# Adaptive-norm chunks moved between TensorE and VectorE, and a wider norm and split before the feed-forward part

## The chip, the cores and the metric

The program runs on one core of a Trainium2 chip. A core has five engines with a queue of instructions each: TensorE (PE; its weight loads are shown apart as PEld), VectorE (DVE), ScalarE (ACT), GpSimd (POOL) and SyncE (SP), which here issues nearly all DMAs. The metric is the device time of one execution in microseconds (us); several executions give a median.

## The reference, cut to what matters

Two layers work on 640 tokens, 512 latents of one request and 128 context tokens of another, with 1024 features each. Layer 0 has two mixers side by side (A, a bidirectional mLSTM, and B, a Hyena long convolution); layer 1 has neighbourhood attention (mixer C). Around each mixer and each feed-forward part stands the same frame:

```
sh1, sc1, gt1, sh2, sc2, gt2 = split(silu(c) @ w_ada[l] + b_ada[l], 6)   # per layer, c or c_ctx
h = rmsnorm(x, g_mix[l]) * (1 + sc1) + sh1
x = x + gt1 * mixer(h)
a, g = split(rmsnorm(x, g_ffn[l]) * (1 + sc2) + sh2) @ w_up[l], 2)
x = x + gt2 * ((gelu(dwconv3(a)) * g) @ w_down[l])
```

The six vectors of a layer are the "chunks" 0 to 5 of this text: shift, scale and gate of the mixer (0, 1, 2), shift, scale and gate of the feed-forward part (3, 4, 5). Each is a product of a 2-row matrix (c and c_ctx) with 1024 x 1024 weights. The feed-forward width is 2816 = 22 tiles of 128. All arithmetic is fp32.

## The kernel before, in words

**Layout.** Features lie on the 128 partitions in 8 tiles, tokens along the free axis, in two halves of 320 (the first is all latents, the second 192 latents and 128 context tokens, so per-request scalars need two instructions there: RANGES[1]). A normed input is held as a high part XH (rounded to fp32r) and a low part XL (the rest); a product is three matmuls, high by high, high by low, low by high.

**The order of the work.** Engines run their queues in order. The order inside a queue is set by a scheduler of the language from the program's order, its own estimates and explicit marks (`tc.issue_after`); it can push an instruction ahead of ones that stand before it in the code. So a part that is added in one place also moves its neighbours.

**Adaptive-norm chunks.** There are two ways to compute one. `ada_pe` (L212) does it on TensorE, in four steps; a step loads two weight tiles `wa` of 512 KB and runs four matmuls, each on 32 columns of the array, into a PSUM tile `ada`; after the fourth step four small matmuls `adaq` turn the result round. `ada_dve` (L242) does it on DVE, in 16 steps; a step loads one tile `adw` of 256 KB and runs two multiply-and-sum instructions, whose unused product is called `adj` and whose sums go to a tile `ada`; the DVE rows called adj are these. Chunks 0 and 1 of layer 0 run at the start on TensorE, chunks 2, 3, 4 in mixers A and B on TensorE, one step after each of twelve projection tiles (`filler()` at L791, which `linear` calls). Chunk 5 of layer 0 (16 DVE steps, list `early`, L1411) runs in the output projection and the norm after it. Chunks 0 and 1 of layer 1 (32 DVE steps, list `steps`) run in the feed-forward part of layer 0, between the tiles of the down projection: the filler in `ffn_s` (L411) issues by turns two steps and one. Chunks 2 to 5 of layer 1 (64 steps, 8 in each of 8 head pairs) run in mixer C with a single `adw` buffer (L1171, L1348).

**The norm before the feed-forward part.** `norm_part` (L312) treats one feature tile of one half. DVE multiplies x by the coefficient and the broadcast rms factor `rb` into a tile `keep`, ACT adds the shift and rounds to XH, DVE forms XL from keep, shift and XH. In the second half each of these runs twice, on 192 and 128 tokens. Since keep has no shift yet, `shift()` (L463) adds it later on ACT.

**The head of the feed-forward part.** The up projection works by a Strassen-like scheme on sums and differences of the four quarters of the normed input (n11, n21, n12, n22 in keep). `sums()` (L470) forms them between the first three pairs of up tiles (`u_0` to `u_5`, whose low parts are `u_0l` and so on, in PSUM tiles `pu`), and `split_t` (L458) splits four of them, T3, T2, T4 and T1, into a high part by ACT and a low part by a DVE subtraction (128 x 1280 elements each). After the head, `up(f)` (L517) makes seven products per tile f (PSUM tiles A, B, C; their split weights are named `w35wl` for product 3 of tile 5, and so on), a product taking its weights from the loaded tiles `u_5a`, `u_5g`. `down()` (L574) runs four times, the last time at the end; its tiles are `pd`, its residual update writes x. A gate tile `G` and its raw form `gg` lie between up and down.

## Time and profile before

| | us |
|---|---|
| median of 3 runs (range) | 1717.03 (1715.11 to 1718.37) |
| the profiled execution | 1717.35 |
| its span in the trace | 1715.6 |
| busy: PE, DVE, ACT, POOL | 1628.6, 1337.8, 798.5, 147.4 |
| mean granted TensorE clock, share of full | 0.986 |

The stages in the trace: 0 to 75 the start, with filters and first norm; 75 to 217 Hyena and the q/k projection; 217 to 366 the mLSTM; 366 to 412 output projection 0; 412 to 475 the norm and the head of feed-forward 0; 475 to 823 the up and down tiles of feed-forward 0; to 905 its last down, the next norm and the first pair's projection; 905 to 1190 mixer C; 1190 to 1240 output projection 1; 1240 to 1310 norm and head of feed-forward 1; 1310 to 1716 the rest of it. A busy share near 1 for PE in a stage says that work added to TensorE there lengthens the stage; a share well below 1 says that something else ends last there, and the rows of waits say what.

### The profile page before, as it was taken

What the parts mean: (1) busy time and instruction counts of PE and PEld (TensorE: products, weight loads), DVE (VectorE), ACT (ScalarE), POOL (GpSimd) and SP (SyncE); (2) the same over time, 40 slices, a digit from 0 to 9 for tenths busy, and PEclk for the clock granted to TensorE, in tenths of its full rate; (3) what the DMA queues carried; (4) which work ended last, traced back from release to release, by engine and by line L of the source; (5) the groups of instructions that cost most, each with busy time, mean ns of one, the idle gap of its engine ahead of it and who ended that gap; (6) DMA issues with size and microseconds to landing.
All of it is one profiled execution on the core that took longest, in us unless ns stands there. A gap on an engine that the chain in (4) does not pass through costs nothing.

```text
span 1715.6 us, 28580 instructions
## 1 busy us (share of the span) xinstructions
PE 1628.6 (95%) x10978; PEld 1538.9 (90%) x10978; DVE 1337.8 (78%) x2894; ACT 798.5 (47%) x1538; POOL 147.4 (9%) x156
## 2 busy tenths in 40 slices
PE   5999999999799999999997999999988999999997
PEld 2699888999799999999986888888988999999997
DVE  5887556688988989899577777887698597886974
ACT  6323346654542525345355555555274244343542
POOL 3110001101000000000023221220010000000001
PEclk9999999999999999999998999999999999999998
DMA  8335422243214243343323333333311232223231
GB/s 326 111 126 180 148 84 62 61 141 118 69 56 154 82 141 98 92 118 86 97 94 94 102 114 120 101 100 90 117 57 57 67 99 74 87 68 105 75 86 62
DMA packets 69657, 176.71 MB, mean 103 GB/s; under 512 B 9024, under 2 KB 18544, under 8 KB 69264
## 3 DMA queue, kind: packets, MB, share of 16 engines
q1 hardware_dynamic: 69328, 174.71, 32.8%
q8 instruction: 86, 1.41, 0.3%
q14 instruction: 51, 0.42, 0.1%
q0 software_dynamic: 192, 0.17, 0.0%
HBM read 170.65 MB, written 4.20 MB: 102 GB/s over the span
## 4 chain that ended last, share of the span: by engine, by line
PE 78%; DVE 13%; DMA 4%; ACT 3%; issue 2%; POOL 0%; SPq 0%; POOLq 0%; DVEq 0%; ACTq 0%
PE pd L127 14%; PE B L514 11%; PE pqk L127 9%; PE C L514 7%; PE A L514 7%; DMA adw<-in_w_adaT 3%; DVE adj L254 3%; PE pop L127 3%; PE pu L127 2%; PE px L127 2%; PE phyb L127 2%; PE po L127 2%; PE pd L121 1%; PE pS L1317 1%; PE ada L222 1%
## 5 line engine op out<-in xcount | busy, mean ns | idle before, releaser
L349 DVE SCALAR_TENSOR_TENSOR x<-pd,mod,x 128x320 f32<-128x320 f32 (+2 forms) x192 | 73.3, 434 | 107.1 <-PE pd L127 97.3
L254 DVE CUSTOM_DVE_ANT_0 adj<-adw,cbc 128x512 bf16<-128x512 f32 x128 | 96.3, 752 | 38.0 <-DMA adw<-in_w_adaT 36.9
L254 DVE CUSTOM_DVE_ANT_0 adj<-adw,cb 128x512 bf16<-128x512 f32 x96 | 66.1, 689 | 9.4 <-DMA adw<-in_w_adaT 8.0
L564 DVE SCALAR_TENSOR_TENSOR fcb<-fca,cwf,fcb 128x641 f32<-128x641 f32 x76 | 67.1, 884 | 3.0 <-ACT fcb L562 2.6
L1319 ACT COPY pTs<-pS 128x384 f32<-128x384 f32 (+1 forms) x80 | 34.1, 435 | 38.9 <-PE pS L1317 38.4
L1200 ACT ACTIVATE s<-s,nm 128x384 f32<-128x384 f32 x64 | 39.2, 613 | 25.9 <-DVE nm L1305 22.8
L1317 PE MATMUL pS<-ident,s 128*128 128x128 f32 x208 | 36.2, 281 | 13.9 <-DVE s L1202 12.9
L562 ACT ACTIVATE fcb<-fca,cwf 128x641 f32<-128x641 f32 x38 | 31.7, 835 | 34.6 <-DVE fca L519 34.4
L436 ACT ACTIVATE fcb<-fcb 128x641 f32<-128x641 f32 x44 | 32.4, 740 | 30.7 <-DVE fcb L564 30.7
L1382 POOL TENSOR_TENSOR fo<-fo,rs 128x320 f32<-128x320 f32 x8 | 6.9, 896 | 445.0 <-ACT rs L1374 445.0
L288 ACT ACTIVATE sqn<-x 128x320 f32<-128x320 f32 x56 | 25.3, 466 | 40.8 <-DVE x L349 31.9
L1202 DVE TENSOR_SCALAR s<-s,nm 128x384 f32<-128x384 f32 (+1 forms) x80 | 42.9, 543 | 1.2
L1280 POOL TENSOR_TENSOR bm<-amask,wr 128x768 f32<-128x768 f32 x16 | 32.9, 2066 | 118.1 <-issue 91.5
L1317 PEld LDWEIGHTS pS<-ident,s 128*128 128x128 f32 x208 | 23.7, 140 | 20.8 <-DVE s L1202 18.7
L519 DVE TENSOR_TENSOR u<-B,s 128x320 f32<-128x320 f32 x76 | 37.1, 488 | 6.6 <-PE B L514 6.1
L431 ACT CAST G<-gg 128x640 fp32r<-128x640 f32 x44 | 32.0, 728 | 19.9 <-DVE gg L519 17.8
L1305 DVE CUSTOM_DVE_ANT_0 s<-pS,bm 128x384 f32<-128x384 f32 x64 | 34.6, 551 | 8.5 <-PE pS L1304 7.8
L103 POOL TENSOR_TENSOR qk00l<-qk,qk00h 128x1024 fp32r<-128x1024 f32 x1 | 2.8, 2766 | 447.5 <-DVE rn L303 447.5
L1297 PE MATMUL pS<-k,q 128*128 128x256 f32 x128 | 31.0, 329 | 7.6 <-DVE k L1233 7.0
L432 DVE TENSOR_TENSOR G<-gg,G 128x640 fp32r<-128x640 f32 x44 | 36.1, 820 | 1.7 <-ACT G L431 1.6
L519 DVE TENSOR_TENSOR gg<-gg,fcb 128x512 f32<-128x512 f32 x76 | 33.8, 487 | 2.8 <-ACT fcb L436 2.4
L289 DVE TENSOR_TENSOR accn<-accn,sqn 128x320 f32<-128x320 f32 x56 | 30.8, 555 | 6.1 <-ACT sqn L288 5.3
(2003 smaller groups left out, 6136.2 us busy)
## 6 DMA issues: line engine op xcount, KB each, us to landing
adw<-in_w_adaT SPq DMA_DIRECT2D x112, 256.0 KB, 2.9
wa<-in_w_ada SPq DMA_DIRECT2D x40, 512.0 KB, 5.0
d<-in_w_down SPq DMA_DIRECT2D x48, 320.0 KB, 2.8
qk<-in_w_qkv SPq DMA_DIRECT2D x24, 512.0 KB, 3.7
d<-in_w_down SPq DMA_DIRECT2D x16, 448.0 KB, 3.3
u<-in_w_up SPq DMA_DIRECT2D x12, 512.0 KB, 3.7
qk<-in_w_ab SPq DMA_DIRECT2D x8, 512.0 KB, 3.6
op<-in_w_oab SPq DMA_DIRECT2D x6, 512.0 KB, 3.6
```

What stands on the lines that cost most here:

```text
L127: pe.matmul(bank(pt, a)[:, : sp_[a][1] - sp_[a][0]], ww[:, kt], xx[:, slice(*sp_[a])], start=(first and n == 0), stop=(last and n == 2))
L254: dve.tensor_tensor_reduce(out=jk, in0=w, in1=cb[:, s, c], op0=ALU.mult, op1=ALU.add, scale=1.0, scalar=0.0, accum_out=got[0][:, k, h, s : ...
L349: r = dve.scalar_tensor_tensor(out=x[:, k, c0:c1], in0=bank(pt, h)[:, c0 - h * HT : c1 - h * HT], scalar=mod[:, l, ch, k, s : s + 1], in1= ...
L432: here[0] = dve.tensor_tensor(out=g[:, 1], in0=pr, in1=g[:, 0].bitcast(F32), op=ALU.subtract).ins
L514: pe.matmul(o, ww[:, k], xx[:, k], start=(first and k == 0 and n == 0), stop=(last and k == 3 and n == 2), skip_group_check=not first)
L519: tt = lambda o, a, b, op: dve.tensor_tensor(out=o, in0=a, in1=b, op=op)
L564: dve.scalar_tensor_tensor(out=o, in0=av[:, d : d + T + 1], scalar=w[j], in1=o, op0=ALU.mult, op1=ALU.add)
L1200: act.activation(out=s, in_=src, func=AF.Exp, scale=-1.0, bias=nm, accum_out=sm)
L1202: return dve.tensor_scalar(out=s, in0=s, scalar1=sm, scalar2=None, op0=ALU.mult).ins
L1305: dve.tensor_tensor_reduce(out=s, in0=pS[:, 0:384], in1=bm[e][:, (0, 1, 1, 2)[i]], op0=ALU.add, op1=ALU.min, scale=1.0, scalar=3.0e38, acc ...
L1317: pe.transpose(pS[:, j * P : (j + 1) * P], s[:, j * P : (j + 1) * P], ident)
L1319: act.copy(out=t[:, : nk * P], in_=pS[:, : nk * P])
```

## The change

It has five parts. (1) In the second half of the norm before the feed-forward part, DVE multiplies x by rb over all 320 tokens, ACT applies coefficient and shift in place on 192 and 128 tokens, ACT copies the 320 to XH, DVE subtracts over 320. keep of that half then carries its shift, and `shift()` is only for the first half. (2) The low parts of T3, T4 and T1 come from ACT writing minus the high part and an accumulating DMA of 640 KB, issued by POOL, adding the source; T2 stays on DVE. (3) The filler of feed-forward 0 issues two steps on each call. (4) Chunk 5 of layer 0 leaves the DVE list `early` and runs as a fourth `ada_pe` chunk in mixers A and B, with one more `filler()` call after q/k tiles 5, 3, 2 and 6. (5) Feed-forward 0 runs chunks 0, 1 and 2 of layer 1 (48 steps, where it had 32), mixer C chunks 3, 4, 5 (48 steps, where it had 64; 6 in a pair, where it had 8).

```diff
     def norm_part(l, which, nrm, a, rb, ks, keep=None):
         n = 2 * l + which
         for k in ks:
+            if keep and a:
+                t = keep[2 + k // 4][:, k % 4]
+                c = slice(HT, T)
+                dve.tensor_tensor(out=t, in0=x[:, k, c], in1=rb[:, :HT], op=ALU.mult)
+                for c0, c1, s in RANGES[1]:
+                    u = t[:, c0 - HT : c1 - HT]
+                    act.activation(out=u, in_=u, func=AF.Identity, scale=coefA[:, n, k, s : s + 1],
+                                   bias=mod[:, l, 3 * which, k, s : s + 1])
+                act.copy(out=XH[:, k, c], in_=t)
+                last = dve.tensor_tensor(out=XL[:, k, c], in0=t, in1=XH[:, k, c].bitcast(F32), op=ALU.subtract)
+                continue
...
         def filler(st=None):
             every[0] += 1
             st = steps if st is None else st
-            for _ in range(1 + every[0] % 2 if st is steps else 2):
+            for _ in range(2):
...
-        def split_t(dst, src):
+        def split_t(dst, src, by_dma=True):
             act.copy(out=dst[0], in_=src)
-            dve.tensor_tensor(out=dst[1], in0=src, in1=dst[0].bitcast(F32), op=ALU.subtract)
+            if by_dma:
+                act.activation(out=dst[1], in_=dst[0].bitcast(F32), func=AF.Copy, scale=-1.0)
+                pool.dma_start(out=dst[1], in_=src, accum_op=ALU.add)
+            else:
+                dve.tensor_tensor(out=dst[1], in0=src, in1=dst[0].bitcast(F32), op=ALU.subtract)
...
-            shift(2)
-            shift(3)
+            shift(0)
             tt(n22, n22, n12, ALU.subtract)
             split_t(T3, n22)
-            shift(0)
             yield
+            shift(1)
             tt(n12, n12, n11, ALU.subtract)
             tt(n11, n22, n11, ALU.add)
-            split_t(T2, n11)
-            shift(1)
+            split_t(T2, n11, False)
...
-            steps = [ada_pe(0, ((ch, 0), (ch, 1)), hw, "adr", 2, modp, "adasb") for ch in (2, 3, 4)]
+            steps = [ada_pe(0, ((ch, 0), (ch, 1)), hw, "adr", 2, modp, "adasb") for ch in (2, 3, 4, 5)]
...
                 linear(W(13 + j), lambda i, pt, _: done_qk(j, pt), f"qk{j}", head=0, filler=filler)
+                if j in (5, 3, 2, 6):
+                    filler()
...
-            steps = [q for ch in (2, 3, 4, 5) for q in ada_dve(1, ch, at, 1, cb)]
+            steps = [q for ch in (3, 4, 5) for q in ada_dve(1, ch, at, 1, cb)]
...
-                        if 1 <= n <= 8:
+                        if 1 <= n <= 6:
...
-                early = ada_dve(0, 5, pools[1], 2, cb)
-                steps = [q for ch in (0, 1) for q in ada_dve(1, ch, pools[1], 2, cb)]
+                steps = [q for ch in (0, 1, 2) for q in ada_dve(1, ch, pools[1], 2, cb)]
```

On TensorE, in the q/k projection, a step of `ada_pe` stood whole between two tiles before (`pqk` are the tiles' PSUM, `wa` the chunk's weights, XH and XL the input):

```order
L127 MATMUL pqk_1668<-XH,qk50l 128x320 x2
L222 MATMUL ada_1725<-wa_1726,csil 32x512
L222 MATMUL ada_1725<-wa_1727,csil 32x512
L222 MATMUL ada_1725<-wa_1726,csil 32x512
L222 MATMUL ada_1725<-wa_1727,csil 32x512
L127 MATMUL pqk_1740<-XH,qk30h 128x320 x2
```

The next step of the changed kernel, 24 matmuls later in the same tile:

```order
L127 MATMUL pqk_1748<-XH,qk30l 128x320 x2
L222 MATMUL ada_1725<-wa_1734,csil 32x512
L127 MATMUL pqk_1748<-XH,qk30h 128x320 x2
L127 MATMUL pqk_1748<-XL,qk30h 128x320 x2
L127 MATMUL pqk_1748<-XH,qk30l 128x320
L222 MATMUL ada_1725<-wa_1735,csil 32x512
L222 MATMUL ada_1725<-wa_1734,csil 32x512
L222 MATMUL ada_1725<-wa_1735,csil 32x512
```

The step is now two groups, of one and of three matmuls, with five matmuls of the tile between. Of the 16 steps of chunks 2 to 5, nine stay whole and seven are split like this.

On DVE, at the end of the first down projection and the begin of the next up tiles, before (the x rows are the residual of the last down tile, the rows L254 are the chunk's steps, `w35wl` is the low part that product 3 of tile 5 waits for):

```order
L349 SCALAR_TENSOR_TENSOR x<-pd_0_7_1_5342,mod,x 128x128
L254 ISA adj_5378,ada_5028<-adw_5376,cb_3448 128x512
L254 ISA ada_5028 128x1
L519 TENSOR_TENSOR u_6a<-ss_6_5426,u_6a 128x512
L254 ISA adj_5380,ada_5028<-adw_5376,cb_3448 128x512
L254 ISA ada_5028 128x1
L507 TENSOR_TENSOR w35wl<-u_5a,w35wh 128x512
```

And in the changed kernel:

```order
L360 SCALAR_TENSOR_TENSOR x<-pd_0_7_1_5288,mod,x 128x128
L530 TENSOR_TENSOR u_6g<-u_6a,u_6g 128x512
L254 ISA adj_5324,ada_4950<-adw_5322,cb_3490 128x512
L254 ISA ada_4950 128x1
L530 TENSOR_TENSOR gg_5_4907<-B_5_4812,s_5_4791 128x320
L254 ISA adj_5326,ada_4950<-adw_5322,cb_3490 128x512
L254 ISA ada_4950 128x1
L530 TENSOR_TENSOR u_6a<-ss_6_5374,u_6a 128x512
L254 ISA adj_5330,ada_4950<-adw_5328,cb_3490 128x512
L254 ISA ada_4950 128x1
L518 TENSOR_TENSOR w35wl<-u_5a,w35wh 128x512
```

Between the last residual and `w35wl` stand three adj where there were two, and `u_6g` and `gg_5` besides; two more adj stand among the three parts of that residual, which had none. Counted from the first adj of this down projection, 31 adj come ahead of `w35wl`, where 22 did.

On DVE, in the head of feed-forward 0, the low part of the fifth up tile, `u_4l`, stood behind two gate products, two gate subtractions and a token sum:

```order
L455 TENSOR_TENSOR gg_0_4374<-pu_1_4221,fcb_4194 128x2x128
L452 TENSOR_TENSOR gg_1_4466<-pu_3_0_4416,fcb_4195 128x320
L452 TENSOR_TENSOR gg_1_4466<-pu_3_1_4417,fcb_4195 128x192
L452 TENSOR_TENSOR gg_1_4466<-pu_3_1_4417,fcb_4195 128x128
L432 TENSOR_TENSOR G_0_4377<-gg_0_4374,G_0_4377 128x640
L472 TENSOR_TENSOR keep_3444<-keep_3447,keep_3444 128x1280
L432 TENSOR_TENSOR G_1_4470<-gg_1_4466,G_1_4470 128x640
L103 TENSOR_TENSOR u_4l<-u_4_4481,u_4h 128x1024
```

In the changed kernel it stands right behind the first gate product:

```order
L466 TENSOR_TENSOR gg_0_4309<-pu_1_4156,fcb_4129 128x2x192
L466 TENSOR_TENSOR gg_0_4309<-pu_1_4156,fcb_4129 128x2x128
L103 TENSOR_TENSOR u_4l<-u_4_4401,u_4h 128x1024
L443 TENSOR_TENSOR G_0_4312<-gg_0_4309,G_0_4312 128x640
L463 TENSOR_TENSOR gg_1_4386<-pu_3_0_4336,fcb_4130 128x320
```

So `gg_1`, both `G` and one sum of 1280 elements moved behind `u_4l`.

## Rows read from the trace of the kernel before

**Rows 1.** Page, part 4: shares of the chain that ended last.

```profile
PE 78%; DVE 13%; DMA 4%; ACT 3%; issue 2%; POOL 0%; SPq 0%; POOLq 0%; DVEq 0%; ACTq 0%
```

**Rows 2.** Stages: window, length, busy (count) of PE, PEld, DVE, ACT, POOL, clock, DMA, GB/s.

```profile
75.00:217.00 142.00, 141.83 (x990) 126.26 (x989) 106.39 (x192) 42.14 (x77) 9.64 (x4) 1.00 0.44 149
412.00:475.00 63.00, 51.39 (x318) 49.03 (x318) 58.22 (x128) 39.12 (x75) 5.11 (x3) 0.95 0.25 76
475.00:823.00 348.00, 346.65 (x2347) 344.04 (x2346) 314.95 (x644) 149.47 (x251) 0.00 (x0) 1.00 0.35 105
905.00:1190.00 285.00, 262.35 (x1965) 238.49 (x1963) 225.67 (x588) 154.03 (x362) 65.05 (x46) 0.98 0.35 107
1240.00:1310.00 70.00, 60.99 (x391) 58.67 (x390) 63.42 (x128) 43.83 (x86) 8.19 (x15) 0.95 0.17 54
```

**Rows 3.** Timeline of PE: start, duration, line, operation, out<-in; TensorE chunk groups.

```profile
49.73 0.31 PE L121 MATMUL phya<-XH,hya0l 128*128 128x320 f32 x1
49.97 1.06 PE L222 MATMUL ada<-wa,csil 128*32 128x512 f32 x6
50.95 0.41 PE L121 MATMUL phya<-XL,hya0h 128*128 128x320 f32 x1
51.20 0.31 PE L118 MATMUL phya<-XH,hya1h 128*128 128x320 f32 x1
...
52.47 1.04 PE L222 MATMUL ada<-wa,csil 128*32 128x512 f32 x2
...
177.20 0.95 PE L230 MATMUL adaq<-selc,adasb 128*128 128x4 f32 x8
```

**Rows 4.** Loads of the tile wa between 75 and 217 us: landing times.

```profile
DMA to landing us min/median/max: 3.5/4.4/6.3
```

**Rows 5.** Timeline of PE in head 0, rows that had idle before them.

```profile
432.99 0.41 PE L118 MATMUL pu<-XH,u_0h 128*128 128x320 f32 x1 [1.88 <-ACT XH L324]
...
462.41 0.56 PE L127 MATMUL pu<-XH,u_4l 128*128 128x320 f32 x2 [4.46 <-DVE u_4l L103]
```

**Rows 6.** First down projection: stage of all engines, then adj alone on DVE.

```profile
511.00:547.00 36.00, 36.00 (x248) 36.00 (x247) 29.05 (x74) 7.17 (x11) 0.00 (x0) 1.00 0.51 151
...
511.00:547.00 36.00, 13.77 (x20) 1.00 0.51 151
```

**Rows 7.** Timeline of the first down and its end: DVE, then PE.

```profile
531.09 0.69 DVE L254 CUSTOM_DVE_ANT_0 adj<-adw,cb 128x512 bf16<-128x512 f32 x1
...
531.83 0.69 DVE L254 CUSTOM_DVE_ANT_0 adj<-adw,cb 128x512 bf16<-128x512 f32 x1
...
549.94 0.69 DVE L507 TENSOR_TENSOR w35wl<-u_5a,w35wh 128x512 fp32r<-128x512 f32 x1
...
550.69 0.41 PE L514 MATMUL C<-XH,w35wl 128*128 128x320 f32 x1
```

**Rows 8.** Page, part 6: DMA issues, KB each, median us to landing.

```profile
adw<-in_w_adaT SPq DMA_DIRECT2D x112, 256.0 KB, 2.9
...
u<-in_w_up SPq DMA_DIRECT2D x12, 512.0 KB, 3.7
```

**Rows 9.** Waits between 905 and 1190 us.

```profile
DVE adj L254 <- DMA adw<-in_w_adaT: 31.8, 24, 3.1
...
PE pS L1317 <- DVE s L1202: 12.9, 16, 1.3
```

**Rows 10.** Timeline of PE in head 1, and the stage behind its wait.

```profile
1293.94 0.90 PE L127 MATMUL pu<-XH,u_4l 128*128 128x320 f32 x2 [4.31 <-DVE u_4l L103]
...
1292.60:1299.40 6.80, 5.46 (x20) 5.46 (x21) 6.80 (x7) 1.97 (x2) 0.00 (x0) 0.50 0.35 91
```

**Rows 11.** ACT cast of T1, and the first matmul of PE that reads its low part.

```profile
473.63 1.26 ACT L459 CAST XH<-keep 128x1280 fp32r<-128x1280 f32 x1 [0.68 <-PE pu L127]
...
484.77 0.30 PE L514 MATMUL C<-XL,w53wh 128*128 128x320 f32 x1
```

**Rows 12.** All DMA issues: the one of 1024 KB.

```profile
cb<-in_cond_b SPq DMA_DIRECT2D x1, 1024.0 KB, 6.4
```

More of the change, by code (lines that the diff above doesn't have):

```diff
@@ L456, in done_up @@
             gate(f, pr)
-        def split_t(dst, src):
+        def split_t(dst, src, by_dma=True):
             act.copy(out=dst[0], in_=src)
-            dve.tensor_tensor(out=dst[1], in0=src, in1=dst[0].bitcast(F32), op=ALU.subtract)
+            if by_dma:
[3 more added lines that the diff above has]
+                dve.tensor_tensor(out=dst[1], in0=src, in1=dst[0].bitcast(F32), op=ALU.subtract)
         def shift(i):
-            a = i // 2
             for k in range(4):
-                for c0, c1, s in RANGES[a]:
-                    t = keep[i][:, k, c0 - a * HT : c1 - a * HT]
-                    act.activation(out=t, in_=t, func=AF.Identity, bias=mod[:, l, 3, 4 * (i % 2) + k, s : s + 1])
+                t = keep[i][:, k]
+                act.activation(out=t, in_=t, func=AF.Identity, bias=mod[:, l, 3, 4 * i + k, 0:1])
         def sums():
@@ L1527, in pack @@
     wa = i["w_ada"]
-    o["w_ada"] = wa[0].reshape(4, 2, P, 6, 2, 512)[:, :, :, :5].transpose(3, 0, 4, 2, 1, 5).reshape(5, 4, 2, P, 1024)
+    o["w_ada"] = wa[0].reshape(4, 2, P, 6, 2, 512).transpose(3, 0, 4, 2, 1, 5).reshape(6, 4, 2, P, 1024)
     o["w_adaT"] = wa.reshape(2, D, 6, KT, P).transpose(0, 2, 3, 4, 1).reshape(12, KT, P, D)[5:]
```

## The prediction

> **What bounds the kernel now.** I read the chain of waits first, then the stages, then the waits inside the stages that the change touches. The chain lies on TensorE for 78% and on DVE for 13% [rows 1]: work added to TensorE should mostly lengthen the run, and work added to DVE should matter where the stage has no slack. The stages say where that is [rows 2]. From 75 to 217 us TensorE is busy 141.83 of 142 us: nothing can be hidden there. From 475 to 823 it is busy 346.65 of 348, but DVE is busy 314.95 as well, so TensorE bounds the stage with DVE some 10% behind. In the two heads (412 to 475 and 1240 to 1310) TensorE stands idle for 63 - 51.39 = 11.6 us and 70 - 60.99 = 9.0 us, and its mean granted clock there is 0.95, worth about 5% of the stage, 3.2 and 3.5 us. In mixer C it is idle for 285 - 262.35 = 22.6 us. So the change takes work out of stages in which TensorE waits, and puts it into a stage in which TensorE bounds and one in which DVE nearly does. The sum is made against the profiled execution, 1717.35 us; the median is 1717.03, so 0.3 is taken off at the end.
>
> **Mixers A and B: a fourth chunk on TensorE.** The rows show what a group of such matmuls costs between two neighbours [rows 3]. From 49.73 to 51.20 pass 1.47 us, in which TensorE also starts two projection matmuls. The first down projection starts 248 matmuls in 36 us, 0.145 apiece [rows 6]; 1.47 - 0.29 = 1.18 us for the group. That group has three matmuls (six records, 1.06 us); the one at 52.47 has a single matmul (two records) and takes 1.04 us. Its size doesn't matter, only the number of groups does, since the four column groups run side by side. Before, chunks 2 to 4 were 12 whole steps, 12 groups. After, the order shows 9 whole steps and 7 that are split in two: 23 groups. 11 x 1.18 = 13.0 us. One more round of adaq (0.95 us busy, overlapping its neighbours a little) adds 0.9: 13.9 in all. Two `wa` buffers hold one step, so the loads of a step start only after the last matmul of the one before. For most of the split steps 24 matmuls lie between, 24 x 0.145 = 3.5 us, and a load lands after 3.5 at best, 4.4 in the median [rows 4]. The first group needs only the first of the two tiles, so I take 0.3 us for each of seven such steps, 2 us; the bounds are 0 and, with the median landing, 7 x 0.9 = 6.3. Term: +15.9, from +13.9 to +20. Nothing covers it.
>
> **Norm and head of feed-forward 0.** The ceiling is 11.6 + 3.2 = 14.8 us. The DVE steps of chunk 5 leave this stage, and with them the delay in XH and XL for which TensorE waits (1.88 us in one place [rows 5]). The largest wait, 4.46 us for `u_4l` [rows 5], gets shorter as `gg_1`, two G and one sum move behind `u_4l`. It doesn't go: `gg_0`, still ahead of it, needs the gelu on ACT, and ACT has the negation of T3 to do first, 1.26 us if it is as long as the cast of T1 [rows 11]. I leave 1.8 us of it, and 2.9 for idle of other origin (the first wait for the rms factor, a split on POOL). 14.8 - 4.7 = 10.1. Term: -10, from -5 to -13.
>
> **Low parts by accumulating DMA.** No such DMA stands in the trace. For T3 and T4 DVE is relieved. T1 comes last: its cast ran at 473.63 to 474.9 [rows 11], the negation would end at 476.2, and TensorE first reads the low part at 484.77 [rows 11], 8.6 us later. A load of 512 KB lands in 3.7 us [rows 8] and one of 1024 KB in 6.4 [rows 12]; 640 KB lie between, near 4.4, and up to twice that, 8.8, if reading the destination as well costs as much again. If the head gets shorter by 10 us on TensorE, ACT's cast must move with it. Term for both layers: +1, from 0 to +5. The Trainium skill ("DMA: Bandwidth & Descriptors", section "Anatomy of one DMA — SWDGE (gpsimd) path") fits a DMA issued by GpSimd as 2.0 us plus bytes over 436 GB/s, here an estimate of 3.5 us. "Collectives: The Full Stack" of the Trainium skill (section "The bandwidth ceiling: the fold count and why AG ≠ RS ≠ AR") speaks against the change: an adding DMA reads two sources and so pushes twice the read traffic. By the two together T1 would be an estimate of 5 us, still inside the 8.6, and the term would be 0; no row here shows such a DMA.
>
> **The downs of feed-forward 0.** Feed-forward 0 now carries 48 steps, which is 32 adj more. Two adj back to back start 0.74 us apart [rows 7]; 23.7 us of DVE work. DVE has 348 - 315 = 33 us free in the stage as a whole [rows 2], but not where the work comes: in the first down it is busy 29.05 of 36 us, 13.77 of them in 20 adj [rows 6]. The order says when this shows: 31 adj come ahead of `w35wl`, where 22 did, so `w35wl` comes 9 x 0.74 = 6.7 us later, less what of the free 36 - 29.05 = 6.95 us can be used. Before, it ran 549.94 to 550.6 and the matmul that reads it started at 550.69 [rows 7]: just in time, so each us later is a us of TensorE. The bounds are 0 and 6 for a down. That all the free time can be used is not likely: two steps for a tile of 36/8 = 4.5 us need two loads of 2.9 us [rows 8] through two buffers, and a buffer is taken for 2.9 + 2 x 0.74 = 4.4 us and the issue. I take 2.7 for each of three downs (the third gets 16 steps where it had 8). Term: +8, from 0 to +16.
>
> **Mixer C.** A quarter of the steps goes. DVE waited 31.8 us for `adw` there, in 24 waits, and TensorE 12.9 us in 16 for a DVE row `s` that stands behind such waits [rows 9]. A quarter of it would be 3.2 us, all of it 12.9. I take 7, since two units of each pair have no step at all now. Term: -7, from -3 to -13.
>
> **Norm and head of feed-forward 1.** Ceiling 9.0 + 3.5 = 12.5. `u_4l` cost 4.31 us of waiting, and behind it stand 6.8 us at half clock (1.2 GHz), worth 3.4 [rows 10]. With 1.8 left of the wait and the clock kept up, 2.5 + 3.4 = 5.9; the wide norm saves DVE some instructions in front of TensorE: 1 more. Term: -7, from -2 to -10.
>
> **The sum.** 15.9 - 10 + 1 + 8 - 7 - 7 = +0.9; 1717.35 + 0.9 - 0.3 = 1718. Gains and costs, each over 20 us, nearly cancel.
>
> **Rivals.** *The downs hide it.* DVE uses all its free time in the downs (0 in place of +8), the loads of `wa` come in time (+13.9), and the heads and mixer C give -11, -8 and -9: 13.9 - 11 + 0 + 1 - 9 - 8 = -13, 1704. For it speaks the free 33 us of DVE; against it that 0 for a down needs every idle us. *The DVE queue becomes the bound in feed-forward 0* (slower). Place: the three downs and the up tiles behind them. A tile's DVE work is four adj (3.0), a residual and a weight split; if these pass 4.5 us, or a load through two buffers does, each tile lags, and the lag reaches `w35wl` and its like as 5 us each: +15 in place of +8, 1725. It decides from the point at which DVE shows no idle between residuals. For it speaks 13.77 us for 20 adj in 29.05 busy: twelve more leave nothing. *`wa` is late* (slower): the loads of the split steps land after the median 4.4 us or more beside the projection's own loads; +8 to +10 in mixers A and B: 1725 too. *The split groups don't cost*: if a group of one matmul hid beside its neighbours, mixers A and B would cost four groups, one adaq and the waits, 4.7 + 0.9 + 2 = 7.6 in place of 15.9, and the time be 1710; the row at 52.47 speaks against it.
>
> **How the numbers follow.** I give my forecast 0.37, the downs that hide it 0.25, free split groups 0.05, the DVE bound 0.20, late `wa` 0.13. A measurement of this kernel can tell about 0.2%, 3.4 us, from no change. Of the forecast's 0.37 (its own range 1712 to 1724) 0.25 are within that, 0.06 on either side; the first rival and the free groups give 0.28 to faster and 0.02 to same, the two slow ones 0.29 to slower and 0.04 to same. Faster 0.34, same 0.31, slower 0.35. For 8 in 10 the range reaches to the rivals on both sides: 1703 to 1732.
>
> **What would show it.** Between 75 and 225 us the stage should be 14 to 18 us longer, with groups `ada` of x2 and x6 at about 1.05 us each. The head of feed-forward 0 should show `u_4l` waits under 2 us and no clock of 0.5 behind it. After the pd of each down there should be a wait of TensorE for a low part (`w35wl`) of 2 to 4 us; if there is none, the first rival holds; if it is over 4 or DVE is busy over 97% from 475 to 823, the second. In mixer C the wait for `adw` should fall from 31.8 to about 24 us. The prediction fails if the accumulating DMA lands later than 8 us, or if the norm's second half, now with three ACT instructions per tile, makes TensorE wait for ACT where it waited for DVE.

## The result and the profile after

The changed kernel takes 1731.79 us, median of 4 runs (1729.16 to 1733.87), beside 1717.7 us (1715.11 to 1719.31) for the kernel before: a ratio of 1.0083, 95% interval 1.0068 to 1.0099. It is slower by 0.8%, some 14 us. The forecast was 1718, no change, with a range of 1703 to 1732: the median lies 0.2 us inside its upper end. The profiled execution takes 1729.16 us with a span of 1727.4, against 1715.6: 11.8 us more.

Where they went can be read from the starts of named matmuls on TensorE, since the same groups run in both kernels. A stage here is the time from the first start of one group to the first start of the next (us; "head" is output projection, norm and up head together, from `pop` to the first product A):

| stage, from - to | before | after | change | forecast |
|---|---|---|---|---|
| start, to `phya` | 49.04 | 45.87 | -3.2 | 0 |
| mixers A and B, `phya` to `px` | 202.18 | 221.24 | +19.1 | +15.9 |
| mLSTM, `px` to `pop` | 120.92 | 120.93 | 0 | 0 |
| head 0, `pop` to A | 105.11 | 92.61 | -12.5 | -10 |
| A to the first down | 33.80 | 33.90 | +0.1 | +1 (T1) |
| the first three downs, `pd` to A, each | 35.20 | 35.20 | 0 | |
| up tiles behind them | 63.62, 62.47, 78.03 | 69.96, 69.34, 86.77 | +21.9 | +8 |
| last down, projection C | 83.96 | 84.12 | +0.2 | 0 |
| mixer C, `pv` to `pop` | 302.43 | 295.18 | -7.3 | -7 |
| head 1, `pop` to A | 102.58 | 95.65 | -6.9 | -7 |
| feed-forward 1 to the end | 405.82 | 406.23 | +0.4 | 0 |

One row is far off: the up tiles of feed-forward 0. The stages of the changed kernel that answer to [rows 2], in the same columns (window, length, busy time and count of PE, PEld, DVE, ACT and POOL, clock, DMA, GB/s):

```profile
72.00:220.50 148.50, 146.10 (x972) 124.47 (x972) 103.43 (x186) 40.61 (x75) 9.65 (x4) 0.99 0.45 150
428.00:480.60 52.60, 48.91 (x330) 47.83 (x331) 45.51 (x84) 41.42 (x72) 7.24 (x5) 1.00 0.33 85
480.60:846.20 365.60, 350.24 (x2318) 346.56 (x2317) 330.54 (x703) 147.00 (x248) 0.89 (x1) 0.97 0.39 112
930.30:1214.00 283.70, 267.05 (x2003) 242.77 (x2003) 219.51 (x573) 158.40 (x374) 62.87 (x46) 0.98 0.34 102
1255.00:1321.00 66.00, 62.24 (x411) 60.67 (x410) 52.61 (x98) 46.86 (x81) 9.51 (x6) 0.97 0.26 69
```

In the third row TensorE is now idle 365.6 - 350.24 = 15.4 us, where it was idle 1.35, and its clock is 0.97 where it was 1.00. DVE is busy 330.54 of 365.6, 90%, the same share as before: it is not full. So something makes both wait. The timeline of TensorE shows where: once behind each of the first three downs (start, duration, instruction, idle before it and its releaser):

```profile
559.26 0.63 PE L525 MATMUL B<-TT,w45wh 128*128 128x320 f32 x1 [5.13 <-ACT w45wh L517]
...
663.73 0.90 PE L525 MATMUL B<-TT,w611wh 128*128 128x320 f32 x2 [3.39 <-ACT w611wh L517]
...
769.03 0.90 PE L525 MATMUL B<-TT,w415wh 128*128 128x320 f32 x2 [5.32 <-ACT w415wh L517]
```

The chain of waits between 545 and 565 us of the changed kernel says what ended the first of them (start, duration, what):

```profile
547.67 3.36 DMA adw<-in_w_adaT
551.16 0.69 DVE adj L254
...
553.10 3.01 DMA adw<-in_w_adaT
556.24 0.69 DVE adj L254
557.34 0.49 DVE adj L254
557.95 0.62 DVE u_6a L530
558.59 0.63 ACT w45wh L517
559.26 0.90 PE B L525 x2
```

Read from below: the product waits for ACT's cast, the cast for DVE's row that makes `u_6a`, and that stands behind adj rows which wait for their loads. DVE's own timeline shows these waits (bracketed, as above):

```profile
541.12 0.69 DVE L254 CUSTOM_DVE_ANT_0 adj<-adw,cb 128x512 bf16<-128x512 f32 x1 [1.40 <-DMA adw<-in_w_adaT]
...
551.16 0.69 DVE L254 CUSTOM_DVE_ANT_0 adj<-adw,cb 128x512 bf16<-128x512 f32 x1 [0.65 <-DMA adw<-in_w_adaT]
...
557.87 0.69 DVE L530 TENSOR_TENSOR u_6a<-ss,u_6a 128x512 f32<-128x512 f32 x1
```

There are five of them in this down and the turn behind it, 0.52 + 0.29 + 1.40 + 0.65 + 0.30 = 3.2 us; the other two downs have 3.1 and 3.4 us. Within each wait of TensorE begins a stretch at half clock, which goes on behind it; the stages of these stretches, columns as in [rows 2]:

```profile
556.50:563.30 6.80, 4.04 (x15) 4.04 (x16) 6.46 (x17) 0.71 (x2) 0.00 (x0) 0.50 0.58 175
662.30:669.10 6.80, 5.36 (x19) 4.95 (x20) 5.94 (x19) 4.15 (x7) 0.00 (x0) 0.50 0.32 105
768.10:774.90 6.80, 5.87 (x22) 5.87 (x23) 4.64 (x12) 0.62 (x1) 0.00 (x0) 0.50 0.26 77
```

TensorE is busy 4.04 + 5.36 + 5.87 = 15.3 us in them at 1.2 GHz in place of 2.4, so half of that, 7.6 us, is lost. The idle time grew by about 14.1 us (15.0 us of waits of 0.3 us or more between 546 and 850, less 0.9 in the same place before). 14.1 + 7.6 = 21.7 of the 21.9 us.

In the mixers the groups on TensorE look as [rows 3] let expect, and one load is late:

```profile
188.92 1.05 PE L222 MATMUL ada<-wa,csil 128*32 128x512 f32 x2
190.83 1.06 PE L222 MATMUL ada<-wa,csil 128*32 128x512 f32 x6
...
197.76 1.62 PE L222 MATMUL ada<-wa,csil 128*32 128x512 f32 x2 [2.17 <-DMA wa<-in_w_ada]
```

A group of one matmul (x2: each has two records) and one of three (x6) take the same time. There are 23 groups, as forecast. The last shown ran at half clock (its stretch is 3.4 us long and doesn't stand in the six runs below with the same code, which take 218.8 to 219.3 us for the stage: +17).

In both heads the wait for `u_4l` that [rows 5] and [rows 10] show is down to 1.10 us. No half clock stands behind it in head 0; in head 1 a stretch of 3.4 us does (the last row, columns as in [rows 2]):

```profile
467.64 0.56 PE L127 MATMUL pu<-XH,u_4l 128*128 128x320 f32 x2 [1.10 <-DVE u_4l L103]
...
1306.62 0.56 PE L127 MATMUL pu<-XH,u_4l 128*128 128x320 f32 x2 [1.10 <-DVE u_4l L103]
...
1307.40:1310.80 3.40, 3.40 (x15) 3.40 (x14) 3.40 (x6) 1.94 (x2) 0.00 (x0) 0.50 0.56 154
```

In mixer C the waits that answer to [rows 9] (us in total, times, longest; between 905 and 1225 us) are shorter:

```profile
DVE adj L254 <- DMA adw<-in_w_adaT: 20.9, 23, 1.9
...
PE pS L1330 <- DVE s L1215: 8.9, 13, 1.3
```

And the accumulating DMAs, which no row of before showed, stand in the list of DMA issues with their landing time:

```profile
TT<-keep POOLq DMA_DIRECT2D x4, 640.0 KB, 5.6
XL<-keep POOLq DMA_DIRECT2D x2, 640.0 KB, 6.0
```

The one for T1 of layer 0 is issued at 480.19 and by the median of 6.0 us lands about 486.2; TensorE reads XL of it from 488.27 and waits for nothing.

The 3.2 us at the start are no effect of the change. Stretches of half clock near 36 us come and go there between kernels whose start is the same (before, and the runs e1, e4, e5, e6 and e12 have 6.8 us of it, e7 and e9 have 3.4, the changed kernel and e2, e3, e8 and e11 none). Without the start the traces differ by 15.0 us, near the 14 of the medians.

### The profile page after: what moved, and what is told of

Its sections match the earlier page's. It is cut to its first block, busy times and chain, and to the rows that moved or that the text cites. A ratio compares the mean times of both kernels' runs of the same rounds, so it can differ in the third digit from the quotient of the medians.

```text
span 1727.4 us, 28568 instructions
## 1 busy us (share of the span) xinstructions
PE 1643.4 (95%) x11018; PEld 1543.5 (89%) x11018; DVE 1304.2 (75%) x2792; ACT 804.1 (47%) x1529; POOL 151.1 (9%) x162
## 4 chain that ended last, share of the span: by engine, by line
PE 51%; DVE 14%; DMA 5%; issue 2%; ACT 2%; POOL 0%; POOLq 0%; ACTq 0%; DVEq 0%
PE B L525 11%; PE pd L127 10%; PE C L525 7%; PE A L525 7%; DMA adw<-in_w_adaT 5%; DVE adj L254 4%; PE pqk L127 2%; PE pu L127 2%; PE pu L121 1%; PE pop L127 1%; PE pd L121 1%; DVE s L1215 1%; PE pS L1330 1%; PE py L1345 1%; PE pS L1310 1%
## 5 line engine op out<-in xcount | busy, mean ns | idle before, releaser
L254 DVE CUSTOM_DVE_ANT_0 adj<-adw,cbc 128x512 bf16<-128x512 f32 x96 | 68.6, 715 | 21.8 <-DMA adw<-in_w_adaT 20.9
L254 DVE CUSTOM_DVE_ANT_0 adj<-adw,cb 128x512 bf16<-128x512 f32 x96 | 65.9, 687 | 10.9 <-DMA adw<-in_w_adaT 9.6
L360 DVE SCALAR_TENSOR_TENSOR x<-pop,mod,x 128x320 f32<-128x320 f32 (+2 forms) x36 | 14.3, 433 | 36.7 <-PE pop L127 26.1
L222 PE MATMUL ada<-wa,csil 128*32 128x512 f32 x192 | 39.6, 662 | 2.2 <-DMA wa<-in_w_ada 2.2
```

The lines of the kernel that those rows point to most:

```text
L222: pe.matmul(pt[32 * j : 32 * j + 32, :], cs_[0][:, 2 * kp + par, :], rr[i][:, par * 512 : (par + 1) * 512], start=(kp == 0), stop=(kp == 3))
L254: dve.tensor_tensor_reduce(out=jk, in0=w, in1=cb[:, s, c], op0=ALU.mult, op1=ALU.add, scale=1.0, scalar=0.0, accum_out=got[0][:, k, h, s : ...
L360: r = dve.scalar_tensor_tensor(out=x[:, k, c0:c1], in0=bank(pt, h)[:, c0 - h * HT : c1 - h * HT], scalar=mod[:, l, ch, k, s : s + 1], in1= ...
```

## The experiments

Each was timed 4 to 10 times beside the kernel before on the same chip; ratios are to that kernel, with the 95% interval. The kernel before took 1714.4 to 1717.7 us on these chips, so runs are best compared by their ratios. Stage lengths are from their traces, by the same starts as in the table. All but e1, e3 and e4 have three adw buffers in feed-forward 0, as e2 does.

**e1: the old pace.**

```diff
-            for _ in range(2):
+            for _ in range(1 + every[0] % 2 if st is steps else 2):
                 if st:
```

> The changed kernel with part 3 undone alone: the filler of feed-forward 0 issues two steps and one by turns, so its 48 steps run 12 in each of four downs, the last one included, where the changed kernel puts 16 in each of the first three. Theory (pace): the adj rows of a down stand in DVE's queue ahead of the row that makes u_6a, whose cast TensorE waits for; with 24 adj as in the kernel before they come in time. Then the waits of 5.1, 3.4 and 5.3 us behind the first three downs fall below 0.6 each, the three stretches of half clock behind them go, the up tiles take 62 to 64, 62 to 63 and 78 to 79 us again (from 70.0, 69.4 and 86.8), and the time is about 20 us shorter, 1711. The last down may give back up to 3 us. Rival (load): it is the number of steps in the stage, with its DMA traffic, not the pace: 48 are still there, and most of the 22 us stays, 1727 to 1732.

Measured: 1711.61 us, ratio 0.9981 (0.9968 to 0.9995). The up tiles take 64.1, 61.7 and 79.4 us; the largest wait behind a down is 0.74 us and no half clock stands there. The projection of mixer C, behind the last down that now has steps, takes 35.2 us in place of 31.8: 3.4 us back. The theory held. All 48 steps are still in the stage, so their number is not the cause. The pace is, but this doesn't yet say whether by DVE's work or by the loads.

**e2: three adw buffers, pace as changed.**

```diff
-                steps = [q for ch in (0, 1, 2) for q in ada_dve(1, ch, pools[1], 2, cb)]
+                steps = [q for ch in (0, 1, 2) for q in ada_dve(1, ch, pools[1], 3, cb)]
```

> The changed kernel with three adw buffers in feed-forward 0, where it has two; the pace of two steps for a tile stays. DVE waited for adw in the first down and the turn behind it 0.5 + 0.3 + 1.4 + 0.65 + 0.3 = 3.2 us. Theory (pace): DVE work ahead of u_6a is too long in any case, the loads are a part of it: the waits behind the downs shrink by up to 3 us each but do not go; the time is 4 to 10 us shorter, 1722 to 1728. Rival (loads): the two buffers are the cause, and with three the waits and the half clock behind them go: about 1711.

Measured: 1710.82 us, ratio 0.998 (0.9967 to 0.9993). The up tiles take 64.3, 63.6 and 80.3 us, 4.1 us more than before the change and 17.8 less than with two buffers. In no wait of 0.3 us or more between 475 and 842 does DVE wait for adw. What is left of TensorE's waits behind the first and the third down:

```profile
554.06 0.56 PE L525 MATMUL B<-TT,w45wh 128*128 128x320 f32 x2 [2.40 <-ACT w45wh L517]
...
752.42 0.56 PE L525 MATMUL B<-TT,w415wh 128*128 128x320 f32 x2 [2.39 <-ACT w415wh L517]
```

My theory expected a gain of 4 to 10 us; the rival held. The rows ahead of `u_6a` in DVE's queue cost 2.4 us of wait, which no half clock follows here. The loads cost the rest: 2.7 us more of wait in the first down, 2.9 in the third, and the half clock. A third buffer also changes the order of DVE's queue a little, but not in a way that could explain the gain: 31 adj of the first down stand ahead of `u_6a` in e2, 30 in the changed kernel, and yet `u_6a` starts 5.3 us behind the first product A in e2 and 8.1 in the changed kernel (2.5 before).

**e3: whole groups on TensorE.** The order of the two matmuls that share a half step is turned round.

```diff
-                for i in range(2):
+                for i in (1, 0):
                     j = 2 * par + i
```

> The changed kernel with the two matmuls of each half step of the chunks on TensorE in the other order, so that the first of a step reads the tile that is loaded second; then no step is split, 16 groups where the changed kernel has 23. Theory (number of groups): seven groups less are 7 x 1.18 = 8.3 us; the projection stage, 19 us longer than before in the changed kernel, is 9 to 11 us longer; time 1722 to 1725. Rival (loads): what costs there is waiting for wa, and as a whole step now waits for its second tile, the waits eat the gain: 1728 to 1733.

Measured: 1726.33 us, ratio 1.0069 (1.0046 to 1.0092). All 16 steps are whole, seven groups less, but mixers A and B take 218.9 us, as with split groups. The number of groups alone doesn't set the stage. The stage from `phya` to `px` in the kernel before, e2 and e3, columns as in [rows 2]:

```profile
49.04:251.22 202.18, 202.01 (x1297) 174.15 (x1293) 149.85 (x286) 72.64 (x131) 16.51 (x13) 1.00 0.41 135
...
45.61:264.76 219.15, 216.55 (x1337) 176.48 (x1333) 151.71 (x289) 72.51 (x130) 16.93 (x14) 1.00 0.41 142
...
46.47:265.37 218.90, 210.51 (x1339) 177.28 (x1336) 151.69 (x290) 72.67 (x130) 16.94 (x14) 0.99 0.41 142
```

TensorE's busy time is 6.0 us less in e3 than in e2, and 8.5 less without the 2.5 us that two stretches at half clock cost in e3, close to the 7 x 1.18 = 8.3 us of the seven groups. But its idle time is 8.4 us where e2 has 2.6. It waits three times for wa (1.79, 0.52, 0.57; e2 once, 1.6), and at the stage's end for the gate columns:

```profile
263.28 0.78 PE L990 MATMUL gT<-ident,R 128*128 128x128 f32 x4 [3.71 <-ACT R L978]
```

The gates' first row on ACT, in this kernel, waits for the last Hyena block (`hy`), which stands behind the adaq of the last step:

```profile
240.29 0.80 ACT L934 ACTIVATE gt<-pgates,bgt 128x640 f32<-128x640 f32 x1 [5.11 <-PE hy L875]
```

In the kernel before the same row ran 16 us earlier, and its chain was over before TensorE wanted it. In the changed kernel and in e2 it runs as late as in e3 (243.05 and 240.69), but there TensorE comes to gT later and waits for nothing. So neither expectation holds: the groups' gain is there, and waits that the split groups had hidden take it back. The row of before:

```profile
224.04 0.79 ACT L921 ACTIVATE gt<-pgates,bgt 128x640 f32<-128x640 f32 x1
```

**e4: low parts of the sums on DVE.**

```diff
-        def split_t(dst, src, by_dma=True):
+        def split_t(dst, src, by_dma=False):
```

> The changed kernel with the low parts of T3, T4 and T1 formed by a DVE subtraction again, no accumulating DMA. Theory (the chunk and the wide norm made the heads shorter, the DMA did little): the stretch from output projection 0 to the first product is 92.6 us in the changed kernel, 105.1 before; it gets 1 to 3 us longer; that of layer 1 too (95.7, 102.6 before); time 1733 to 1737. Rival (the DMA gave most of it): each head goes half the way back or more, 5 us and more in sum: over 1738. Second rival (the accumulating DMA costs): it gets faster, below 1730.

Measured: 1727.38 us, ratio 1.0076 (1.0055 to 1.0096), the same as the changed kernel. Head 0 takes 92.5 us, head 1 94.0; 0.7 us is lost behind each head, where TensorE waits 0.45 us for a weight split on DVE. The heads got neither 1 to 3 us longer nor 5 and more. The time is under the 1730 of the second rival, but the kernel before ran 3.3 us shorter here as well (1714.41), and the intervals of the two ratios overlap: the DMAs neither shorten the heads nor cost anything that these runs can tell.

**e5: narrow norm** (part 1 undone: `norm_part`, `shift` and `sums` as before, with the DMAs).

> The changed kernel with three adw buffers in feed-forward 0 and with part 1 undone: the norm's second half in narrow steps again, with the shift of keep added later. Theory (the steps that left shorten the heads): the stretch from output projection to the first product stays within 2 us of the changed kernel's 92.6 and 95.7, and the time within 3 us of the version with three buffers alone. Rival (the wide norm does it): both stretches go back by 3 us or more each, most of the way to 105.1 and 102.6, and the time is 6 us longer or more.

Measured: 1712.23 us, ratio 0.9969 (0.9956 to 0.9983). Heads 94.4 and 95.9, within 2 us. The first theory held.

**e6: chunk 5 on DVE** (part 4 undone).

```diff
-            steps = [ada_pe(0, ((ch, 0), (ch, 1)), hw, "adr", 2, modp, "adasb") for ch in (2, 3, 4, 5)]
+            steps = [ada_pe(0, ((ch, 0), (ch, 1)), hw, "adr", 2, modp, "adasb") for ch in (2, 3, 4)]
...
-                if j in (5, 3, 2, 6):
-                    filler()
...
+                early = ada_dve(0, 5, pools[1], 3, cb)
```

> The changed kernel with three adw buffers in feed-forward 0 and with part 4 undone: chunk 5 of layer 0 runs on DVE in output projection 0 and its norm again. Theory (chunk 5 costs on TensorE what groups, waits and the end of the chain cost, and gives back the head's gain): mixers A and B take 202 us again, 17 less; the stretch behind them goes back from 92.6 to 101 to 105, 8 to 12 more; the time is 5 to 9 us shorter than with three buffers alone. Rival (the wide norm and the DMA have taken over the head's gain): the stretch stays near 93 and the time is 15 us shorter or more.

Measured: 1695.86 us, ratio 0.987 (0.9849 to 0.989), by its median the fastest of all. That is 15 us below e2, the time of the rival, where the theory had 5 to 9; the profiled executions are 10.5 us apart. Mixers A and B take 202.2 us, 17 less; head 0 takes 98.8, 6.2 more, between the two expectations. `u_4l` keeps its early place, and the waits for XH, 2.6 us in two, come back:

```profile
455.74 0.74 PE L127 MATMUL pu<-XH,u_4l 128*128 128x320 f32 x2 [1.09 <-DVE u_4l L103]
```

**e7: whole groups, and the additional steps early.**

```diff
-                if j in (5, 3, 2, 6):
+                if j in (0, 1, 4, 7):
                     filler()
```

> The changed kernel with three adw buffers in feed-forward 0, the whole groups of the run with that name, and the four additional fillers after q/k tiles 0, 1, 4 and 7 instead of 5, 3, 2 and 6, so that the last step of chunk 5 comes where chunk 4's last step came before. In the run with whole groups alone, TensorE waited 3.7 us for the gate columns (gT): the gates' first row on ACT waits for the last Hyena block, which stands behind the last step's adaq. Theory (the end of the chain): with the last step early, that chain starts 15 us or more earlier and is hidden; mixers A and B take 208 to 213 us (219 to 221 in the changed kernel), the time is 6 to 11 us shorter than with three buffers alone. Rival (the loads of wa): two steps in one tile wait for their loads wherever they stand; 216 to 219, and the time stays.

Measured: 1700.93 us, ratio 0.9903 (0.9886 to 0.9919). Mixers A and B take 209.5 us, 9.6 less than in e2; `gt` starts at 228.66, 12 us earlier than in e2 and e3, and gT waits for nothing. The stage, columns as in [rows 2]:

```profile
46.36:255.87 209.51, 207.07 (x1339) 175.44 (x1335) 151.09 (x289) 74.06 (x132) 16.62 (x14) 1.00 0.44 148
```

The first theory held in the length of the stage; the time is 10 us under e2 by the medians and 13 by the ratios, where 6 to 11 were expected. Against e2 the gain is busy time, 9.5 us, that is the groups, at the same idle time of 2.4 to 2.6 us. Against e3, which has whole groups too, the early place alone gives 9.4 us: it takes away the waits. Split groups in the early place weren't tried. Against the 202.2 of before the chunk costs 7.3 us here: four groups and one adaq, 5.1 us of busy time (5.6 by the prices of the forecast), and waits.

**e8: chunk 2 of layer 1 back in mixer C** (part 5 undone).

```diff
-            steps = [q for ch in (3, 4, 5) for q in ada_dve(1, ch, at, 1, cb)]
+            steps = [q for ch in (2, 3, 4, 5) for q in ada_dve(1, ch, at, 1, cb)]
...
-                        if 1 <= n <= 6:
+                        if 1 <= n <= 8:
...
-                steps = [q for ch in (0, 1, 2) for q in ada_dve(1, ch, pools[1], 3, cb)]
+                steps = [q for ch in (0, 1) for q in ada_dve(1, ch, pools[1], 3, cb)]
```

> The changed kernel with three adw buffers and with part 5 undone: feed-forward 0 has 32 steps, mixer C 64 in 8 for each pair. Theory (a quarter of the steps): mixer C takes 300 to 303 us again (295 to 296 with 48 steps), and as its last steps run into output projection 1 and the norm, that stretch goes back to 101 to 103 from 95.7; feed-forward 0 gets 2 to 5 us shorter, and the time is 5 to 11 us longer than with three buffers alone. Rival (the wide norm shortened head 1): mixer C goes back, but the stretch behind it stays at 94 to 96, and the time is 1 to 5 us longer.

Measured: 1722.13 us, ratio 1.0038 (1.0019 to 1.0056), 0.6% above e2's ratio, some 10 us, as the theory had it. Its ten runs spread over 12 us, and the profiled one is the fastest. Mixer C takes 302.4 us again, to 0.1 us what it took before. Head 1 takes 99.1, between the two expectations: 18 adj run in it, as the steps spill over into output projection 1 (before the change 18 too, none in the changed kernel), and TensorE waits 1.7 us for XL and 0.9 for XH there as it did before, but for `u_4l` only 1.1 us. The wait for adw in mixer C goes back as well:

```profile
DVE adj L254 <- DMA adw<-in_w_adaT: 33.4, 25, 3.0
```

**e9: e6 with three steps on a call in output projection 0.**

```diff
         def filler():
-            for _ in range(2):
+            for _ in range(3):
                 if steps:
```

> The version with three adw buffers and chunk 5 on DVE, with one more edit: the filler of output projection 0 issues three steps on a call instead of two, so that more of chunk 5's 16 steps come before the norm. In that version TensorE still waits 1.8 + 0.4 + 0.8 us for XH and XL in head 0. Theory (adj rows left in the norm make these waits): the stretch from output projection 0 to the first product falls from 98.8 us to 95 to 97, the time by 2 to 4 us. Rival (three steps delay the residuals of the output projection, as two through two buffers did in the downs): the stretch gets longer, 99 to 103, and the time by up to 4 us.

Measured: 1698.43 us, ratio 0.9897 (0.9877 to 0.9917), which overlaps e6's interval. Head 0 takes 97.5, 1.25 less, in part because a new wait comes up, 2.02 us of TensorE for the sum of squares on DVE. That is in neither expected range; inconclusive in time, no gain.

**e11: parts 1 and 2 both undone** (e5 with `by_dma=False`).

> The changed kernel with three adw buffers in feed-forward 0, and parts 1 and 2 both undone: narrow norm, all low parts of the sums on DVE. In the runs with one of them undone TensorE waited 1.0 us for u_4l (4.5 and 4.3 before the change, 1.1 with it). In the order of this kernel u_4l still stands right behind the first gate product. Theory (u_4l's place in DVE's queue sets its wait, and parts 1 and 2 matter little for it): it waits 1 to 2 us in both layers, the two stretches up to the first product take 93 to 96 and 95 to 98 us, the time stays within 4 us of the version with three buffers alone. Rival (the DVE work that part 1 or part 2 takes away shortens u_4l, either being enough): with both undone it waits over 3 us again, with half clock behind it, and the stretches take 97 us and more, 99 and more.

Measured: 1714.54 us, ratio 0.9996 (0.9981 to 1.0011). Heads 93.0 and 93.0, as short as with both parts (behind each, as in e4, 0.7 us is lost). The wait for `u_4l` in head 0:

```profile
466.00 0.56 PE L127 MATMUL pu<-XH,u_4l 128*128 128x320 f32 x2 [1.02 <-DVE u_4l L103]
```

The theory held, and head 1 is even shorter than the 95 to 98 expected. Its span, 1706.9 us, is that of e2 (1707.1); its timed runs spread more widely, over 9.8 us.

**e12: parts 1, 2 and 4 undone** (the edits of e6 and e11 together).

> The changed kernel with three adw buffers in feed-forward 0 and with parts 1, 2 and 4 undone: what is left is the pace of two steps and the other split of layer 1's chunks. Chunk 5's steps are in head 0 again, and there u_4l stands behind the second gate product and both G as before the change; in head 1 it stands right behind the first. Theory (the heads get shorter if either the chunk's steps leave or parts 1 and 2 are there; the place of u_4l carries it): the stretch up to the first product takes 103 to 106 us in layer 0 with a wait of about 4.5 us for u_4l, 93 to 96 in layer 1 with one of about 1; mixers A and B take 202; the time is 4 to 8 us more than with chunk 5 on DVE and parts 1 and 2 (ratio 0.987). Rival (parts 1 and 2 do nothing in any case): layer 0 takes 98 to 100 as there, and the time is the same.

Measured: 1707.78 us, ratio 0.9953 (0.9935 to 0.9971). Head 0 takes 105.25 us, to 0.2 us what it took before the change, with its waits:

```profile
433.31 0.42 PE L118 MATMUL pu<-XH,u_0h 128*128 128x320 f32 x1 [2.48 <-ACT XH L324]
436.41 0.63 PE L118 MATMUL pu<-XH,u_0h 128*128 128x320 f32 x1 [1.51 <-ACT XH L324]
...
461.92 0.90 PE L127 MATMUL pu<-XH,u_4l 128*128 128x320 f32 x2 [4.46 <-DVE u_4l L103]
```

Head 1 takes 96.1 with a wait of 1.0 for `u_4l`. The theory held for the stages. In time it didn't: the ratio is 0.8% above that of e6, 12 to 14 us, where 4 to 8 us were expected. The traces are 9.6 us apart, 6.5 of them in head 0, 2.0 in head 1 and 0.8 behind it. The rival, the same time as e6, is out.

The two heads by what stands in them, then, in us:

| | parts 1 and 2 | neither |
|---|---|---|
| head 0 with chunk 5's DVE steps in it | 98.8 (e6) | 105.3 (e12; before 105.1) |
| head 0 without steps | 92.6 (changed, e2) | 93.0 (e11) |
| head 1 with the last 18 adj of mixer C in it | 99.1 (e8) | 102.6 (before) |
| head 1 without | 95.7 (changed), 94.1 (e2) | 93.0 (e11), 96.1 (e12) |

Both heads say the same: the steps that leave make the head short by themselves; parts 1 and 2 help only where steps are left.

## Why the prediction was right or wrong

**The step that failed** is the term of the downs: "I take 2.7 for each of three downs ... Term: +8, from 0 to +16". It measured +21.9, outside its own bounds, and it is nearly all of the difference between the forecast and the result. The mechanism was named: more adj ahead of a row that TensorE waits for, just behind the down (the row was `u_6a`, three rows ahead of `w35wl`, by way of ACT's cast). Its size had three parts, and I priced one. With the loads in time (e2) the longer queue costs 4.1 us in all, half of the 8. The loads and the clock cost the other 17.8: two steps for a tile through two buffers left DVE waiting 3.1 to 3.4 us in each down. I had worked out that a buffer is taken for 4.4 us "and the issue", against a tile of 4.5, and then used it only to say that not all free time could be used, not as a wait that each row behind it in the queue inherits. And the clock: I charged half clock in head 1 from [rows 10], but not behind the waits that I forecast here; that is 7.6 us in three stretches. e1 and e2, which take away one cause each of the late loads, both bring 17 to 18 us back (e1 20.8 in the up tiles, less 3.4 in the next projection).

**The range.** That 1731.79 lies in the range is owed to its width and to luck, not to the sum: the forecast's own range was 1712 to 1724, no rival was priced far above 1725, two of the four executions took 1733.34 and 1733.87, and the one term of the downs was 14 us out.

**The rivals.** The second rival, which I gave 0.20, was the nearest. Its place was right, its 5 us for each down are near the 5.1, 3.4 and 5.3 measured, and its condition names what happened: "if these pass 4.5 us, or a load through two buffers does, each tile lags". Of its two signs one came true (a wait over 4 us, in two of the three downs); the other did not: DVE was to be without idle, busy over 97%, and it is busy 90%, as it waits for loads. Its price of +15 left out the clock. The first rival, nothing for a down, is out. Late `wa` gave one wait of 2.2 us, and free split groups are out by the 14.5 us of busy time below.

**Mixers A and B**, +15.9 forecast, +19.1 in the profiled execution and +17 in six other runs of the same code: right in size and in its account. From before to e2 TensorE's busy time in the stage grew by 216.55 - 202.01 = 14.5 us, where 13.9 was forecast for eleven groups and one adaq, and its idle time by 2.4, where 2 was; 1.6 of that is one wait for `wa`. In the changed kernel that wait is 2.2 us and half clock behind it costs 1.7 more. What I had not seen costs nothing here but stands in the way of a gain: the end of the chunk holds up the last Hyena block and by it the gate chain, which takes some 23 us from `gt` to gT (240.29 to 263.28 in e3). I read the count in the PE order and not the Hyena block behind adaq. Whole groups alone (e3) make TensorE wait for that chain; whole and early (e7) they save 9.6 of the 17 us.

**Head 0**, -10 forecast, -12.5 measured, and the wait for `u_4l` fell under 2 us as forecast. Of the causes, the chunk's steps that leave head 0 are enough alone (105.3 to 93.0); parts 1 and 2 bring 6.5 where the steps stay and 0.4 where they leave. The forecast's mechanism, the place of `u_4l`, is borne out: TensorE waits 1.0 to 1.1 us for it wherever it stands right behind the first gate product (changed kernel, e6, e8, e11) and 4.3 to 4.5 where both `G` stand ahead of it (before, e12). What I had wrong is what moves it there: the relief of DVE by the DMAs does not matter once the steps are gone. Why the scheduler puts `u_4l` early if either is done was not tried.

**Head 1**, -7 forecast, -6.9 measured: the sum came out by luck, its terms did not. The clock was to give 3.4 us and gave 1.1. [rows 10] show TensorE busy 5.46 of the 6.8 us, so no more than half of that, 2.7, was there to be won, and 3.4 us at half clock still stand behind `u_4l`. The idle time was to fall by 3.5 us, 2.5 at `u_4l` and 1 by the wide norm, and fell by 5.2 (102.5 - 93.53 to 95.7 - 91.93): 3.2 at `u_4l` and 2.6 in the waits for XL and XH, less 0.6 that other waits grew. The waits for XL and XH go with the 18 adj of mixer C's last steps (e8 has both again), which I had not seen in this head. The wide norm shows nothing once they are gone (93.0 without it in e11).

**Mixer C**, -7 forecast, -7.3 measured; e8 puts the steps back and has 302.4 again. Its wait for adw fell from 31.8 to 20.9 us, by a third, where a quarter of the steps went and 24 was expected.

**The accumulating DMAs**, +1 forecast, nothing measured. 5.6 to 6.0 us lie inside the bounds of 4.4 to 8.8 that [rows 8] and [rows 12] gave, and T1 came 2.1 us before its reader. The Trainium skill ("DMA: Bandwidth & Descriptors", section "Anatomy of one DMA — SWDGE (gpsimd) path") gave an estimate of 3.5 us, which the trace exceeds by 60% and more. With the second read that "Collectives: The Full Stack" of the Trainium skill names for the adding step of a collective (section "The bandwidth ceiling: the fold count and why AG ≠ RS ≠ AR") the estimate was 5 us, nearer; the measured value decides.

**Of the change as a whole**: parts 1 and 2 do next to nothing once the steps have left the heads; part 5 gains in mixer C and head 1 but needs room in feed-forward 0, which a third buffer gives; part 4 moves some 24 us of DVE work (32 adj at 0.74) that cost 6 to 12 us where it was to a place where it costs 17, or 7.3 if its groups are whole and early (e7). The version that keeps parts 1, 2, 3 and 5, with a third adw buffer (e6), is 1.3% faster than the kernel before; e7, with all five parts, is 1.0% faster, and their intervals touch, so which of the two is better stays open.

## What to carry to other kernels

When work that waits for its own loads is put more densely into an in-order queue, work out the period of its buffers (load, use and issue) against the time that one period of the loop gives it, and charge a shortfall to everything that stands behind it in that queue, with the clock that a longer wait of TensorE costs besides. A third buffer, or a slower pace, is worth trying before anything is moved. And when steps are added at the end of a stage, follow not only their own cost but what is queued behind the last of them: it can be hidden at first and then take back what a cheaper step would gain, as in e3.

## What the runs showed of the hardware

With waits of TensorE of 5.13, 3.39 and 5.32 us went 6.8 us each at a granted clock of 0.5; behind waits of 2.40 and 2.39 us in the places of the first and third (e2) it stayed at 1. But the wait alone doesn't decide: in the changed kernel the same wait of 1.10 us for `u_4l` was followed by no half clock in head 0 and by 3.4 us of it in head 1. In the changed kernel a group of one matmul on 32 columns of the array took 1.05 us, and one of three, each on 32 other columns, 1.06. An accumulating DMA of 640 KB within SBUF landed after 5.6 to 6.0 us (medians), beside 3.6 for the plain loads `u` of 512 KB in the same run.
